# A two-layer hybrid encoder on eight cores: all engines ordered by a list scheduler, a token-major residual, linear chunked retention, a block form of the 31-tap convolution, and feed-forward groups of 512

## The chip, the cores and the metric

The kernel runs on all eight cores of one Trainium2 chip. Every core works on two of the sixteen sequences and runs the same program; no core talks to another. The metric is the device time of the slowest core in microseconds (us).

Executions come in states. In many of them some cores, often a pair or a whole die (cores 0 to 3 are die 0, 4 to 7 are die 1), are granted a lower TensorE clock than the others for some milliseconds, and the run is longer. Such a run is called slow; a run in which no die was held back is called fast. In a slow run the other die is often undisturbed. Two kinds of number are therefore compared in this text: fast runs with fast runs, and the spans of the cores of an undisturbed die. The runs were made on several chips. Undisturbed dies of the kernel before took about 12390 to 12450 us on all of them, so the spans can be compared across chips. The engines are PE (TensorE), DVE (VectorE), ACT (ScalarE), POOL (GpSimd) and SP (the queue that issues most transfers).

## The reference, cut to what matters

```python
D_MODEL, SEQ, DEPTH, CHUNK, D_FF = 1024, 2048, 2, 64, 4096     # 16 sequences in all

def hybrid_mixer(h, ...):
    q, k, v, g_ret, sc_b, sc_c, sc_x, cf_in, gate_logits = jnp.split(h @ w_in, split_at, axis=-1)
    # A: retention, 4 heads, keys 128 wide, values 256 wide. Weight of key m for query n:
    #    gamma_h^|n-m| in the same chunk of 64, gamma_h^(n-m) for earlier chunks, 0 for later ones
    o = head_norm(chunkwise_retention(rotary(q), rotary(k), v))
    y_a = (silu(g_ret) * o) @ w_ret_o
    # B: short gated convolution, 3 taps
    y_b = (sc_b * causal_depthwise_conv(sc_c * sc_x, sc_conv_w)) @ w_sc_o
    # C: conformer module: GLU, depthwise convolution of 31 taps, layer norm, silu
    u = causal_depthwise_conv(glu_a * sigmoid(glu_b), cf_dw_w) + cf_dw_b
    y_c = silu(layer_norm(u)) @ w_cf_o
    return (g0 * y_a + g1 * y_b + g2 * y_c) @ w_o               # g: sigmoid gates per channel

for l in range(DEPTH):
    x = x + 0.5 * rms_norm(swiglu_ffn(rms_norm(x, g[0]), ffn1_w_gu[l], ffn1_w_down[l]), g[1])
    x = x + rms_norm(hybrid_mixer(rms_norm(x, g[2]), ...), g[3])
    x = x + 0.5 * rms_norm(swiglu_ffn(rms_norm(x, g[4]), ffn2_w_gu[l], ffn2_w_down[l]), g[5])
```

Inputs and outputs are float32. Both kernels multiply in bfloat16 and accumulate in float32.

## The kernel before

The kernel is written by hand, one stage after the other. Each engine executes its instructions in the order in which the program makes them. Activations are kept feature-major (channels on the partitions, tokens along the rows), so a sum over channels needs a matmul with a matrix of ones. The parts that the argument touches:

```python
# sum of squares over channels: ACT squares, PE adds over the partitions with ones
def ssq_bank(srcs):
    pb = bank()
    for i, (ap, b) in enumerate(srcs):
        sq = sqbuf()                                              # two buffers
        P.op("act", lambda e: e.activation(out=sq.ap, in_=ap, func=AF.Square), ...)      # line 283
        P.mm_group([lambda pe: pe.matmul(pb.ap, lhsT=ONESB.ap, rhs=sq.ap, ...)], ...)    # line 284
    return pb

# feed-forward in 16 groups of 256 hidden channels; gate_up of the next step is issued before down of this one
for i, (g, t) in enumerate(steps):
    if i + 1 < len(steps):
        g2, t2 = steps[i + 1]
        gate_up(i + 1, g2, t2, wts[g2][0], wts[g2][1])
    down(i, g, t, wts[g][2])        # 8 banks, each added to the sum by DVE, 128x512 (line 379)
    if g == NG - 1:
        postnorm_tile(...)          # residual, sum of squares, and the next block's norm, at once

# retention: every pair of a 128-key tile and a 512-query tile; q and k are also projected a second
# time with their halves swapped, for the rotary embedding
for ib in range(T):
    for jt in range(4 * ib + 4):
        ...   # scores 128x512, DVE multiplies by the decay table, two matmuls with V

# 31-tap convolution: one diagonal 128x128 weight per tap
P.mm_group([(lambda pe, k=k: pe.matmul(pcv.ap, lhsT=DG[:, k, :], rhs=UG[:, t*TT+k:t*TT+k+TT],
                                       start=(k == 0), stop=(k == 30))) for k in range(31)], ...)  # line 731
```

The residual is transposed in float32 on entry (line 807) and on exit (line 822).

Of the kernel before, what the change touches and what calls it, by code (L numbers as in the profile page):

```python
# [10 lines left out]
ALU = mybir.AluOpType  # L11

S = 2048
D = 1024
C = 8
T = 4
TT = 512
NSEQ = 2
# [4 lines left out]
DK = 128  # L23
O_Q, O_K, O_V, O_GR, O_SCB, O_SCC, O_SCX, O_GA, O_GB, O_GATE = 0, 512, 1024, 2048, 3072, 4096, 5120, 6144, 7168, 8192
BIGD = 1.0e5

P_NG = 0
P_SCW = P_NG + L * 6 * C
P_CFW = P_SCW + L * 3 * C
P_CFB = P_CFW + L * 31 * C  # L30
P_LNG = P_CFB + L * C
# [4 lines left out]
NPAR = P_ID + 128  # L36
# [6 lines left out]
class Buf:  # L43
    __slots__ = ("w", "r", "dsem", "dcnt")

    def __init__(self):
        self.w = None
        self.r = {}
        self.dsem = None
        self.dcnt = 0  # L50

class TB:
    __slots__ = ("ap", "b")

    def __init__(self, ap, b=None):
        self.ap = ap
        self.b = b if b is not None else Buf()

class XSt:
    __slots__ = ("ap", "bs")  # L60

    def __init__(self, ap):
        self.ap = ap
        self.bs = [Buf() for _ in range(C)]

class Prog:
    def __init__(self, nc):
        self.nc = nc
        self.engs = {"pe": nc.tensor, "dve": nc.vector, "act": nc.scalar, "pool": nc.gpsimd, "sp": nc.sync}
        self.sem = {k: nc.alloc_semaphore(f"s_{k}") for k in self.engs}  # L70
        self.cnt = {k: 0 for k in self.engs}
        self.waited = {k: {} for k in self.engs}
        self.nsem = 0
        self.dma_toks = []

    def _wait(self, e, tok):
        sem, val = tok
        if e == "pe" and sem is self.sem["pe"]:
            return
        key = id(sem)  # L80
        if self.waited[e].get(key, 0) >= val:
            return
        self.engs[e].wait_ge(sem, val)
        self.waited[e][key] = val

    def deps(self, e, reads, writes):
        for b in reads:
            if b.w is not None:
                self._wait(e, b.w)
        for b in writes:  # L90
            if b.w is not None:
                self._wait(e, b.w)
            for t in b.r.values():
                self._wait(e, t)

    def commit(self, tok, reads, writes):
        k = id(tok[0])
        for b in reads:
            o = b.r.get(k)
            if o is None or o[1] < tok[1]:  # L100
                b.r[k] = tok
        for b in writes:
            b.w = tok
            b.r = {}

    def op(self, e, fn, reads=(), writes=()):
        self.deps(e, reads, writes)
        ins = fn(self.engs[e])
        self.cnt[e] += 1
        ins.then_inc(self.sem[e], 1)  # L110
        tok = (self.sem[e], self.cnt[e])
        self.commit(tok, reads, writes)
        return tok

    def mm_group(self, fns, reads=(), writes=()):
        e = "pe"
        self.deps(e, reads, writes)
        ins = None
        for fn in fns:
            ins = fn(self.engs[e])  # L120
        self.cnt[e] += 1
        ins.then_inc(self.sem[e], 1)
        tok = (self.sem[e], self.cnt[e])
        self.commit(tok, reads, writes)
        return tok

    def dma(self, q, out, in_, reads=(), writes=()):
        self.deps(q, reads, writes)
        tgt = writes[0] if writes else reads[0]
        if tgt.dsem is None:  # L130
            tgt.dsem = self.nc.alloc_semaphore(f"d{self.nsem}")
            self.nsem += 1
        tgt.dcnt += 16
        self.engs[q].dma_start(out=out, in_=in_).then_inc(tgt.dsem, 16)  # L134
        tok = (tgt.dsem, tgt.dcnt)
        self.commit(tok, reads, writes)
        self.dma_toks.append(tok)
        return tok

    def retire(self, bufs):  # L140
        toks = []
        for b in bufs:
            if b.w is not None:
                toks.append(b.w)
            toks += list(b.r.values())
        for e in self.engs:
            for t in toks:
                self._wait(e, t)

    def barrier(self):  # L150
        toks = [(self.sem[k], self.cnt[k]) for k in self.engs if self.cnt[k] > 0] + self.dma_toks
        for e in self.engs:
            for t in toks:
                self._wait(e, t)
        self.dma_toks = []

def build(nl=L, nseq=NSEQ, stop=None):
# [5 lines left out]

    x_d = din("x", [NSEQ, S, D])
    pos_d = din("pos", [NSEQ, S], I32)
    par_d = din("par", [128, NPAR])
    wtab_d = din("wtab", [128, 1408])
    wd = {n: din(n, WSHAPES[n]) for n in WNAMES}
    out_d = nc.dram_tensor("out", [NSEQ, S, D], F32, kind="ExternalOutput").ap()
    xs_d = nc.dram_tensor("xs", [NSEQ, C, 128, S], F32, kind="Internal").ap()  # L170
    xsb = [[Buf() for _ in range(T)] for _ in range(NSEQ)]
    outb = [[Buf() for _ in range(T)] for _ in range(NSEQ)]
# [5 lines left out]
    Hb = [[Buf() for _ in range(T)] for _ in range(C)]  # L178
    RA = sb("RA", [128, 16384], F32)
    ACC = RA.rearrange("p (c n) -> p c n", c=C)  # L180
    RAb16 = RA.bitcast(BF16)
    M = RAb16[:, 0:16384].rearrange("p (c n) -> p c n", c=C)
    U = RAb16[:, 16384:32768].rearrange("p (c n) -> p c n", c=C)
    ACCb = [[Buf() for _ in range(T)] for _ in range(C)]
    Mb = [[ACCb[c // 2][(c % 2) * 2 + t // 2] for t in range(T)] for c in range(C)]
    Ub = [[ACCb[4 + c // 2][(c % 2) * 2 + t // 2] for t in range(T)] for c in range(C)]
    R2 = sb("R2", [128, 8192], F32)
    R2b16 = R2.bitcast(BF16)
    NSLOT = 6
    RING = sb("RING", [128, NSLOT, 2048], BF16)  # L190
    ringb = [Buf() for _ in range(NSLOT)]
    XST = XSt(sb("XST", [128, C, TT], F32))
    PAR = TB(sb("PAR", [128, NPAR], F32))
    WTAB = TB(sb("WTAB", [128, 1408], F32))
    DTAB = TB(sb("DTAB", [128, 1408], F32))
    IDB = TB(sb("IDB", [128, 128], BF16))
    ONESB = TB(sb("ONESB", [128, 128], BF16))
    SQ = [TB(sb(f"SQ{i}", [128, TT], BF16)) for i in range(2)]
    HNB = [TB(sb(f"HNB{i}", [128, TT], BF16)) for i in range(4)]
    ST = [TB(sb(f"ST{i}", [128, TT], F32)) for i in range(4)]  # L200
    AC = [TB(sb(f"AC{i}", [128, TT], F32)) for i in range(3)]
    ACTB_raw = [sb(f"ACTB{i}", [128, 2, TT], BF16) for i in range(2)]
    ACTBb = [[Buf(), Buf()] for _ in range(2)]
    PT = [TB(ACTB_raw[0][:, 0, :], ACTBb[0][0]), TB(ACTB_raw[0][:, 1, :], ACTBb[0][1]), TB(ACTB_raw[1][:, 0, :], ACTBb[1][0])]
    PS = [TB(nc.alloc_psum_tensor(f"ps{i}", [128, TT], F32).ap()) for i in range(8)]

    all_out = []
    ctr = {"bank": 0, "sq": 0, "st": 0, "ac": 0, "pt": 0, "ring": 0}
    rot = {"banks": list(range(8))}

    def bank():
        lst = rot["banks"]
        i = lst[ctr["bank"] % len(lst)]
        ctr["bank"] += 1
        return PS[i]

    def rotbuf(lst, key):
        i = ctr[key] % len(lst)
        ctr[key] += 1
        return lst[i]  # L220

    def sqbuf():
        return rotbuf(SQ, "sq")

    def stbuf():
        return rotbuf(ST, "st")

    def acbuf():
        return rotbuf(AC, "ac")

    def ptbuf():
        return rotbuf(PT, "pt")

    def pcol(off):
        return PAR.ap[:, off:off + 1]
# [4 lines left out]
    IDENT = PAR.ap[:, P_ID:P_ID + 128]  # L240

    P.dma("sp", PAR.ap, par_d, writes=[PAR.b])
    P.dma("sp", WTAB.ap, wtab_d, writes=[WTAB.b])
    P.op("dve", lambda e: e.tensor_copy(out=IDB.ap, in_=IDENT), reads=[PAR.b], writes=[IDB.b])
    P.op("dve", lambda e: e.memset(ONESB.ap, 1.0), writes=[ONESB.b])

    def wslot():
        i = ctr["ring"] % NSLOT
        ctr["ring"] += 1
        return i  # L250
# [4 lines left out]
    def load_unit(pieces, a, bcols):  # L255
        i = wslot()
        view = RING[:, i, 0:a * bcols].rearrange("p (a b) -> p a b", a=a)
        for (c0, n, src) in pieces:
            P.dma("pool", view[:, :, c0:c0 + n], src, writes=[ringb[i]])
        return TB(view, ringb[i])  # L260

    def proj(w, col0, t, pb, src=H, srcb=Hb):
        P.mm_group([
            (lambda pe, k=k: pe.matmul(pb.ap, lhsT=w.ap[:, k, col0:col0 + 128], rhs=src[:, k, tsl(t)],  # L264
                                       start=(k == 0), stop=(k == C - 1)))
            for k in range(C)], reads=[w.b] + [srcb[k][t] for k in range(C)], writes=[pb.b])
# [38 lines left out]
    def load_x(seq, t, xst=None):  # L305
        xst = xst or XST
        if xst is XST:
            carve(XST.bs, "XST")
# [626 lines left out]
```

## Time and profile before

| what | before |
|---|---|
| timed runs at the start | 12808, 13064, 13017 us, median 13017 |
| profiled execution, slowest core | 12585.9 us; die 0 12404 to 12421, die 1 12548 to 12586 at a lower clock |
| PE busy | 88% |
| DVE busy, ACT busy | 52%, 23% |
| 512-wide matmuls in the program | 47104 |
| 256-wide matmuls; float32 transposes | 2048; 512 |

These are the lines of the page of the kernel before that show the limit: the span, the busy time of the engines, the busy tenths of PE in forty slices of the span, and the chain of waits that ended last, as shares of the span by engine.

```profile
span 12585.9 us, 150523 instructions; the slowest of 8 cores (12403.9 to 12585.9 us)
...
PE 11053.0 (88%) x48695; PEld 4960.2 (39%) x49664; DVE 6505.7 (52%) x10794; ACT 2872.7 (23%) x4545; POOL 750.9 (6%) x884
...
PE   4988898899898899889689889988989988998897
...
PE 82%; DVE 7%; ACT 5%; issue 3%; DMA 2%; DVEq 0%; ACTq 0%; SPq 0%; POOL 0%; another core or an unknown queue 0%; POOLq 0%
```

The chain runs through PE for 82% of the span. A busy PE is not yet a PE at full rate, however. The next view has stretches of 200 us of the kernel before: busy time of each engine with the number of its instructions, then the granted TensorE clock (1.00 is full), the share of the DMA engines and GB/s. Weight loads (PEld) are counted completely, so they tell the rate.

```profile
core 4: us, PE busy (x) PEld busy (x) DVE busy (x) ACT busy (x) POOL busy (x), PEclk, DMA share, GB/s
800.00:1000.00 200.00, 145.31 (x558) 57.63 (x567) 129.03 (x202) 69.68 (x107) 13.88 (x16) 0.80 0.43 89
2600.00:2800.00 200.00, 199.05 (x911) 90.66 (x927) 119.15 (x194) 23.32 (x39) 12.36 (x15) 1.00 0.30 39
3000.00:3200.00 200.00, 158.60 (x646) 65.84 (x657) 129.96 (x205) 59.73 (x92) 8.48 (x12) 0.85 0.37 85
```

In the middle of a feed-forward block (2600 to 2800 us) 927 weight loads pass in 200 us: 215.7 ns for each 512-wide matmul. This is the same as the Trainium skill gives for one matmul ("TensorE: Matmul & The Clock Gate", Back-to-back issue gap: N/2.4 + 2.5 ns), and here it is the sustained rate. Where a block ends (800 and 3000 us) only 567 and 657 pass: PE idles and its granted clock is down too, at 0.80 and 0.85.

The waits of PE in the kernel before name who is to blame. The columns are: who waits, for whom; us in total, times, the longest. This is core 4, the slowest.

```profile
PE ps L284 <- ACT SQ L283: 667.0, 519, 19.7
PE ps L471 <- ACT SQ L470: 125.8, 21, 10.1
PE ps L372 <- ACT AC L362: 122.5, 16, 8.0
PE ps L607 <- DVE ACTB L603: 120.8, 67, 7.1
```

The largest is the sum of squares for the RMS norm: ACT squares one 128x512 piece and PE adds it, in turns. On core 0, which belongs to the undisturbed die, all waits of PE add up to 1420 us.

Two groups of the kernel before matter later. Columns: line, engine, operation, output and inputs, count; busy us and mean ns; idle time before and who ended it.

```profile
L379 DVE TENSOR_TENSOR RA<-ps,RA 128x512 f32<-128x512 f32 x3840 | 2333.6, 678 | 0.0
...
L731 PE MATMUL ps<-R 128*128 128x512 bf16 x3880 | 895.3, 385 | 34.7 <-DVE R L723 29.2 <-issue 0.9
```

The first is the sum over feed-forward groups on DVE, the second the convolution on PE (3968 in the program; some matmul records are missing).

### The profile page before, as it was taken

The page shows a single profiled execution, that of the slowest core. Times are in us where ns is not written, and L with a number is a line of the kernel's source. Part 1 is how long each engine was busy: PE and PEld are TensorE (multiplying, and loading weights), DVE is VectorE, ACT ScalarE, POOL GpSimd, SP SyncE. Part 2 cuts the span into 40 slices and gives each one's busy share as a digit, 9 for nine tenths or more (in the row PEclk, how much of TensorE's full clock was granted, in tenths as well). Part 3 has the DMA queues.
Part 4 walks back from the last instruction along what each step waited for, and adds up shares of the span by engine and source line. Part 5 has one row for each costly group of instructions (what it writes and reads, how often), then busy time and mean ns, then how long its engine had stood idle before and what let it go on. Part 6 is the DMA issues. An engine that isn't in the chain of part 4 may idle for free.

```text
span 12585.9 us, 150523 instructions; the slowest of 8 cores (12403.9 to 12585.9 us)
## 1 busy us (share of the span) xinstructions
PE 11053.0 (88%) x48695; PEld 4960.2 (39%) x49664; DVE 6505.7 (52%) x10794; ACT 2872.7 (23%) x4545; POOL 750.9 (6%) x884
## 2 busy tenths in 40 slices
PE   4988898899898899889689889988989988998897
PEld 2434443344343444334334334433434433443343
DVE  1666443456566653445456664335556665424455
ACT  2123212311212311331221331133131133113212
POOL 0000010000000010000000001000000000100000
PEclk7999999899998999989899899998989989898887
DMA  4323231333333232233332323223223232312222
GB/s 105 45 54 46 31 36 12 74 41 51 64 44 72 27 33 24 26 78 74 86 55 43 72 27 33 25 26 74 39 70 50 44 56 31 36 14 37 61 36 62
DMA packets 936848, 602.28 MB, mean 48 GB/s; under 512 B 475040, under 2 KB 786336, under 8 KB 936096
## 3 DMA queue, kind: packets, MB, share of 16 engines
q0 software_dynamic: 816896, 335.60, 23.3%
q1 hardware_dynamic: 119200, 257.00, 6.0%
q8 instruction: 430, 7.05, 0.2%
q14 instruction: 322, 2.64, 0.1%
HBM read 810.64 MB, written 117.44 MB: 74 GB/s over the span
## 4 chain that ended last, share of the span: by engine, by line
PE 82%; DVE 7%; ACT 5%; issue 3%; DMA 2%; DVEq 0%; ACTq 0%; SPq 0%; POOL 0%; another core or an unknown queue 0%; POOLq 0%
PE ps L264 54%; PE ps L372 14%; PE ps L731 6%; ACT SQ L283 2%; PE ps L284 2%; PE ps L558 2%; PE ps L607 2%; DVE AC L338 1%; DVE R L341 1%; DMA RING<-w_in 1%; PE ps L585 1%; DVE ACTB L603 1%; DMA XST<-x 1%; DVE AC L740 1%; ACT L649 0%
## 5 line engine op out<-in xcount | busy, mean ns | idle before, releaser
L264 PE MATMUL ps<-H,RING 128*128 128x512 bf16 x27100 | 6315.9, 388 | 35.6 <-DMA RING<-w_in 3.3
L264 PEld LDWEIGHTS ps<-H,RING 128*128 128x128 bf16 x27648 | 2755.5, 100 | 3427.7 <-issue 502.7
L379 DVE TENSOR_TENSOR RA<-ps,RA 128x512 f32<-128x512 f32 x3840 | 2333.6, 678 | 0.0
L372 PE MATMUL ps<-ACTB,RING 128*128 128x512 bf16 x8052 | 1896.6, 387 | 131.0 <-ACT AC L362 122.5
L364 DVE TENSOR_TENSOR ACTB<-ps,AC 128x512 bf16<-128x512 f32 x1024 | 706.2, 691 | 2316.0 <-PE ps L264 2225.2
L362 ACT ACTIVATE AC<-ps 128x512 f32<-128x512 f32 x1024 | 609.6, 597 | 4154.8 <-PE ps L264 4145.0
L372 PEld LDWEIGHTS ps<-ACTB,RING 128*128 128x128 bf16 x8192 | 810.5, 99 | 1131.8 <-issue 253.0
L284 PE MATMUL ps<-SQ,ONESB 128*128 128x512 bf16 x747 | 353.7, 483 | 683.7 <-ACT SQ L283 667.0
L731 PE MATMUL ps<-R 128*128 128x512 bf16 x3880 | 895.3, 385 | 34.7 <-DVE R L723 29.2
L264 PE MATMUL ps<-RA,RING 128*128 128x512 bf16 x3000 | 741.6, 388 | 47.5 <-ACT RA L744 43.3
L731 PEld LDWEIGHTS ps<-R 128*128 128x128 bf16 x3968 | 390.3, 98 | 519.6 <-issue 86.9
L603 DVE SCALAR_TENSOR_TENSOR ACTB<-ps,DTAB 128x512 bf16<-128x512 f32 x640 | 412.9, 689 | 252.2 <-PE ps L585 139.9
L134 POOL DMA_DIRECT2D RING<-w_in x384 | 336.2, 877 | 3295.3 <-PE ps L264 1544.2
L607 PE MATMUL ps<-ACTB,R 128*128 128x512 bf16 x1252 | 394.4, 403 | 124.9 <-DVE ACTB L603 120.8
L723 DVE TENSOR_TENSOR R<-ps,AC 128x512 bf16<-128x512 f32 x128 | 88.1, 691 | 800.9 <-ACT AC L722 800.7
L134 POOL DMA_DIRECT2D RING<-ffn_w_gu x256 | 227.6, 890 | 4558.7 <-PE ps L264 4466.5
L497 ACT ACTIVATE AC<-ps 128x512 f32<-128x512 f32 x384 | 228.8, 597 | 1109.4 <-PE ps L264 1109.3
L264 PEld LDWEIGHTS ps<-RA,RING 128*128 128x128 bf16 x3072 | 305.3, 99 | 422.3 <-issue 104.7
L284 PEld LDWEIGHTS ps<-SQ,ONESB 128*128 128x128 bf16 x768 | 77.2, 101 | 953.1 <-issue 945.7
L503 DVE TENSOR_TENSOR AC<-ps,AC 128x512 f32<-128x512 f32 x256 | 176.9, 691 | 531.9 <-ACT AC L497 531.9
L338 DVE SCALAR_TENSOR_TENSOR AC<-RA,PAR,ST 128x512 f32<-128x512 f32 x384 | 286.6, 746 | 246.0 <-ACT ST L275 157.2
L712 DVE TENSOR_SCALAR R<-IDB,PAR 128x128 bf16<-128x128 bf16 x992 | 260.5, 263 | 106.4 <-DVE R L712 4.8
(108 smaller groups left out, 6242.9 us busy)
## 6 DMA issues: line engine op xcount, KB each, us to landing
RING<-ffn_w_gu POOLq DMA_DIRECT2D x256, 512.0 KB, 8.0
R<-xs SPq DMA_DIRECT2D x44, 2048.0 KB, 12.8
xs<-R SPq DMA_DIRECT2D x40, 2048.0 KB, 8.0
RING<-w_in POOLq DMA_DIRECT2D x288, 256.0 KB, 4.5
RING<-ffn_w_down POOLq DMA_DIRECT2D x128, 512.0 KB, 5.2
XST<-xs SPq DMA_DIRECT2D x12, 2048.0 KB, 10.1
XST<-x SPq DMA_DIRECT2D x8, 2048.0 KB, 15.5
RING<-w_in POOLq DMA_DIRECT2D x32, 512.0 KB, 7.3
```

The source lines that it names most:

```text
L134: self.engs[q].dma_start(out=out, in_=in_).then_inc(tgt.dsem, 16)
L264: (lambda pe, k=k: pe.matmul(pb.ap, lhsT=w.ap[:, k, col0:col0 + 128], rhs=src[:, k, tsl(t)], start=(k == 0), stop=(k == C - 1)))
L284: P.mm_group([lambda pe, sq=sq, i=i: pe.matmul(pb.ap, lhsT=ONESB.ap, rhs=sq.ap, start=(i == 0), stop=(i == n - 1))], reads=[sq.b, ONESB.b] ...
L338: P.op("dve", lambda e, ap=ap, tmp=tmp, c=c: e.scalar_tensor_tensor(out=tmp.ap, in0=ap, scalar=pcol(P_NG + (l * 6 + ni) * C + c), in1=rs.a ...
L362: P.op("act", lambda e, sg=sg, pg=pg: e.activation(out=sg.ap, in_=pg.ap, func=AF.Silu), reads=[pg.b], writes=[sg.b])
L364: P.op("dve", lambda e, sg=sg, pu=pu, jj=jj: e.tensor_tensor(out=ACTB_raw[ai][:, jj, :], in0=pu.ap, in1=sg.ap, op=ALU.mult), reads=[pu.b, ...
L372: (lambda pe, jj=jj: pe.matmul(pd.ap, lhsT=wdv.ap[:, jj, c * 128:(c + 1) * 128], rhs=ACTB_raw[ai][:, jj, :], start=(jj == 0), stop=(jj == 1)))
L379: P.op("dve", lambda e, pd=pd: e.tensor_tensor(out=ACC[:, c, tsl(t)], in0=pd.ap, in1=ACC[:, c, tsl(t)], op=ALU.add), reads=[pd.b, ACCb[c][ ...
L603: P.op("dve", lambda e, ps=ps, pt=pt, tab=tab, sc=sc: e.scalar_tensor_tensor(out=pt.ap, in0=ps.ap, scalar=float(sc), in1=tab, op0=ALU.mult ...
L607: (lambda pe, e_=e_, pt=pt: pe.matmul(OB[e_].ap, lhsT=VH[:, jt, e_ * 128:(e_ + 1) * 128], rhs=pt.ap, start=(jt == 0), stop=(jt == njt - 1)))
L712: P.op("dve", lambda e, k=k: e.tensor_scalar(out=DG[:, k, :], in0=IDB.ap, scalar1=pcol(P_CFW + (l * 31 + k) * C + c), scalar2=None, op0=AL ...
L731: (lambda pe, k=k: pe.matmul(pcv.ap, lhsT=DG[:, k, :], rhs=UG[:, t * TT + k:t * TT + k + TT], start=(k == 0), stop=(k == 30)))
```

## The change

The intent is to do less on PE and to have PE wait less. Nearly all of the kernel is new:

- **Order.** Operations are recorded first, with a planned duration and a place ("key") counted in PE time. A list scheduler then simulates all engines and buffer pools and issues on each engine what can start first, up to 60 us ahead of the oldest matmul that is left. Buffers are given out by the scheduler.
- **Residual.** It is token-major, so that ACT makes sums of squares along the row. bfloat16 transposes on PE turn the normed tile over; the matmuls with ones for the RMS norm and the float32 transposes go.
- **Retention.** Linear in the sequence: scores only inside a tile of 512 tokens, and a state carried from tile to tile. The second projection of q and k goes; DVE reads the swapped half instead.
- **Convolution.** 16 channels times 8 phases form a block of 128 rows, so that 31 taps are 5 block matmuls of 256 columns. The data goes to DRAM and comes back in this order, before and after.
- **Feed-forward.** 8 groups of 512 hidden channels in place of 16 of 256, and the sum is done 1024 wide.

The diff, cut to its core (the cuts are marked):

```diff
-        for jt in range(njt):                    # retention: all earlier key tiles
-            ps = s_banks.pop(jt)
-            P.op("dve", ... out=pt.ap, in0=ps.ap, scalar=float(sc), in1=tab, ...)
-            P.mm_group([... pe.matmul(OB[e_].ap, lhsT=VH[:, jt, ...], rhs=pt.ap, ...)])
+        psd = PS.tile(f32v(4, 128))              # scores within the tile of 512
+        ...
+        fns.append(lambda pe: pe.matmul(po.v[:, r, :], lhsT=qk.v[:, 0, ...], rhs=st.v..., ...))   # state
+        ...
+        P.op("dve", ... out=ns.v[:, 0:256], in0=st.v[:, 0:256], scalar=float(g512), in1=pst.v, ...)
 ...
-    (lambda pe, k=k: pe.matmul(pcv.ap, lhsT=DG[:, k, :], rhs=UG[:, t*TT+k:...])) for k in range(31)
+    P.op("dve", ... out=ug.v[:, :, t*64:(t+1)*64].rearrange("a p n -> a n p"),
+         in0=th.v.rearrange("a (n p) -> a n p", p=8), ...)                             # line 979
+    P.dma_op("sp", [scr1_d[c] <- ug]); P.dma_op("sp", [X <- scr1_d[c], 8 phases on the partitions])
+    (lambda pe, d=d: pe.matmul(pc.v[:, gi, :], lhsT=W.v[:, d, ...], rhs=X.v[:, g, 4-d:260-d])) for d in range(5)
 ...
+    P.op("act", ... out=u.v[...].rearrange("a (n p) -> a p n", p=8),                   # line 1041
+         in_=tmp.v[...].rearrange("a (p n) -> a p n", p=8), func=AF.Silu, ...), c_act(TT, 2), ...)
 ...
-        NG = DFF // 256
+        NG = DFF // 512
+        P.op("dve", ... out=ACC[:, b, :], in0=pd.v, in1=ACC[:, b, :], op=ALU.add)      # 128x1024, line 713
 ...
-            postnorm_tile(l, seq, npost, t, ...)
+            P.lag = 6.0
+            boundary(seq, b, ...)      # norm, residual, next norm; recorded 6 us later than its place
+            P.lag = 0.0
 ...
+    def _can(self, o, t, old, front):
+        if o.i != old and o.key > front + o.win:      # win is 60 us for computing instructions
+            return None
+        ...
+    P.schedule()
+    P.emit()
```

The scheduler takes an ACT instruction as 0.2 us + columns/1200, with 0.09 us more for each per-partition operand, and a DVE instruction as (150 + columns)/960 us.

## The prediction

> What bounds it now. The core is bound by the tensor engine and by the gaps in it. In the chain of waits PE holds 82% of the span of 12586 us, DVE 7%, ACT 5%. The windows show what a full stretch is: 927 weight loads in 200 us at clock 1.00, so 215.7 ns for a 512-wide matmul (the Trainium skill, "TensorE: Matmul & The Clock Gate", Back-to-back issue gap, has N/2.4+2.5 ns, the same); a burst of 32 256-wide ones took 3.7 us, 116 ns each. From the program: 47104 512-wide, 2048 256-wide and 512 float32 transposes (about 0.2 us): 10.16+0.24+0.10 = 10.50 ms. So about 2.1 ms of this core's span is no full-rate matmul work. The waits of PE give 1.45 ms of idling: 667 us on the squares of the RMS norm, about 570 us more on retention, layer norm, input and output transposes. The rest is a lower clock after gaps (windows at FFN ends: 0.80 to 0.85, 550 to 650 loads in 200 us) and a throttle on pairs of cores (4 and 5 after 10800 us, 6 and 7 early). DVE is busy 52%, DMA about 30%: neither bounds.
>
> What the change does to PE (counted in the built program). Swapped q/k projections go; retention becomes linear in chunks (S^2 scores gone); conv31 falls from 3968 512-wide matmuls to 1280 256-wide; ones-matmuls for RMS sums are replaced by 1536 128-wide bf16 transposes; float32 transposes go. Left: 38144 512-wide, 6528 256-wide, 64 384-wide, 2624 128-wide (I estimate 65 ns): 8.23+0.75+0.01+0.17 = 9.16 ms. All of the 1.34 ms saved is on the critical path.
>
> Gaps: sums of squares go to ACT with accumulation, each block's norm overlaps the next block's matmuls, and the order is chosen for all engines together. I expect 2.1 ms of losses to shrink to 0.4-0.6: start 50, retention 4x50 (many short groups, PSUM of 8 banks), layer norm tiles 16x10 (they fetch 128-byte pieces, 8192 per tile: at the 57 ns per packet that the software queue's 23.3% share implies, 29 us on 16 engines against some 45 us of matmuls), FFN ends 8x10.
>
> DVE: the FFN accumulation drops from 3840x678 ns = 2.33 ms to 896 1024-wide adds, estimated 1.22 us each (158+1067 ns): 1.1 ms. With norm, weight building and head scaling I estimate 5.0 ms in all. ACT about 2.2 ms. Neither is critical, except in the last FFN group (22 us DVE against 20.7 us PE per tile).
>
> Time. 9.16 + 0.5 = 9.7 ms undisturbed on the chip. Timed runs of before were 12.8 to 13.06 ms, 2 to 4% over its profile, so I add the throttle: the same page says the die falls to 13/16 under dense all-core matmuls; this trace shows it only part of the time. A quarter of the matmul work at 13/16 costs 9.16x0.23x0.25 = 0.5 ms; a denser kernel should meet it at least as often. Predicted 10150 us, range 9650 to 10950. Faster by over 2%: 0.97; within 2%: 0.02; slower: 0.01.
>
> What would show it: 47.2 thousand weight loads; full windows still at 927 loads; PE's waits below 400 us; no window at FFN ends under 0.9 clock; retention stage under 300 us per pass; DVE near 5.0 ms. Wrong if: windows at 0.81 cover most of the span (then 11 ms or more); layer-norm fetches take over 45 us per tile; the static order, made with modelled durations, stalls PE where a real DMA is later; 128-wide transposes cost over 100 ns.

## The result, and the profile after

| | runs (us) | median | fast runs |
|---|---|---|---|
| before | 12808, 13064, 13017, 12561, 12438, 12980 | 12893.8 | 12561.5, 12437.5 |
| after | 10207, 10739, 9931, 10203, 9922, 9939 | 10071.2 | 9931.0, 9921.5, 9939.2 |

The ratio of fast runs is 0.7945, with a 95% interval of 0.785 to 0.804. Ratios in this text are the mean time of one kernel's fast runs over the mean of the other's fast runs of the same rounds, so they are not quite the ratio of the medians that are quoted. The two fast runs of the kernel before differ by 1% here. On another chip, later, the ratio was 0.7989 (0.7955 to 0.8023), from fast runs before of 12420.0 and 12428.8 us; that is the cleaner figure. The spans of undisturbed dies are 12404 to 12421 us before and 9909 to 9930 us after.

These are the same lines of the page of the changed kernel.

```profile
span 9930.0 us, 121598 instructions; the slowest of 8 cores (9909.0 to 9930.0 us)
...
PE 9272.8 (93%) x47232; PEld 4541.0 (46%) x47232; DVE 4692.7 (47%) x5226; ACT 2620.8 (26%) x3807; POOL 1005.6 (10%) x1268
...
PE   8998998899999899799999989979999989897999
...
PE 82%; DVE 6%; ACT 5%; issue 4%; DMA 3%; POOL 1%; DVEq 0%; ACTq 0%; another core or an unknown queue 0%; SPq 0%; POOLq 0%
```

PE is busy 93% instead of 88%, in a span that is 2.5 ms shorter than that of an undisturbed core before. The chain has the same 82% of PE as before; it is a share of a shorter span, and it says that there is still something to be had.

How much of the gain is less work, and how much fewer losses? The page and the program give both, with the times of one matmul that the traces show at full clock: 215.7 ns for 512 columns, 109 ns for 256 (a burst of 32 took 3.49 us) and 55 ns for a transpose of 128 (8 took 0.44 us).

| | before | after |
|---|---|---|
| 512-wide | 47104 x 215.7 ns = 10.16 ms | 38144 x 215.7 ns = 8.23 ms |
| 256-wide | 2048 x 109 ns = 0.22 ms | 6528 x 109 ns = 0.71 ms |
| the rest | 512 float32 transposes, about 0.1 ms (estimate) | 64 of 384 and 2624 of 128: 0.15 ms |
| full-rate work | 10.49 ms | 9.09 ms |
| undisturbed span | 12.41 ms | 9.92 ms |
| losses (the difference, unrounded) | 1.93 ms | 0.83 ms |

So work fell by 1.39 ms and losses by 1.10 ms. Of the losses, PE's waits fell from 1420 to 644 us on core 0. Most of the rest is a lower granted clock while PE works: on core 0 the clock records of the traces hold only 1.00 and 0.50, with 0.50 for 1726 us before and 601 us after, and where PE was busy this cost 0.38 and 0.12 ms. It falls in the same stretches as the waits, as the windows of the changed kernel show. Columns are as before.

```profile
core 7: us, PE busy (x) PEld busy (x) DVE busy (x) ACT busy (x) POOL busy (x), PEclk, DMA share, GB/s
600.00:800.00 200.00, 169.36 (x922) 87.42 (x921) 120.01 (x131) 67.13 (x97) 34.08 (x46) 0.91 0.50 119
1600.00:1800.00 200.00, 149.27 (x720) 68.31 (x720) 102.57 (x131) 130.40 (x133) 16.11 (x23) 0.86 0.24 73
2000.00:2200.00 200.00, 199.91 (x925) 89.87 (x924) 69.58 (x57) 19.46 (x19) 14.07 (x17) 1.00 0.37 48
```

The middle of a feed-forward block is as before (924 loads at clock 1.00). The end of a block (600 to 800 us) is at 0.91 in place of 0.80 to 0.85. The weakest stretch is new: 1600 to 1800 us is the layer norm of the conformer branch, with PE busy 149 of 200 us. The waits of PE in the changed kernel say why:

```profile
PE ps L909 <- ACT F L1041: 277.5, 16, 19.7
PE ps L637 <- DVE F L634: 131.4, 41, 15.0
PE ps L996 <- DMA F<-scr: 90.6, 28, 4.2
```

Line 1041 is the Silu after the layer norm, 634 is the scaled tile that PE then transposes at the end of a block, and the third is the convolution's data on its way back from DRAM. Together they are 500 us of the 639 us on this core, core 7. The 16 waits for Silu are one in each of the 16 tiles (four tiles in each of four mixer passes), up to 19.7 us. One tile, on PE in the timeline (start, us, engine, line, what; in brackets the idle time before it and who ended it):

```profile
1611.72 16.50 PE L909 MATMUL ps<-F,RING 128*128 128x512 bf16 x64 [12.90 <-ACT F L1041]
```

and on ACT in the timeline of the same stretch:

```profile
1596.23 9.44 ACT L1041 ACTIVATE F<-F,PAR 128x512 bf16<-128x512 f32 x4
```

Four Silu instructions take 9.44 us. The groups of the changed kernel show that these are out of the ordinary, as is one on DVE:

```profile
L713 DVE TENSOR_TENSOR RA<-ps,RA 128x1024 f32<-128x1024 f32 x896 | 1095.9, 1224 | 748.5 <-PE ps L705 748.1
...
L1041 ACT ACTIVATE F<-F,PAR 128x512 bf16<-128x512 f32 x128 | 331.9, 2670 | 22.0 <-DVE F L1038 14.5 <-DVE SM L625 1.8
...
L979 DVE SCALAR_TENSOR_TENSOR F<-F,ps 128x512 bf16<-128x512 f32 x128 | 310.8, 2428 | 43.8 <-ACT F L978 38.1 <-DVE F L979 0.5
```

Line 713 is the sum over feed-forward groups: 896 times 1224 ns in place of 3840 times 678 ns, less than half. Lines 1041 and 979 write 512 columns of two bytes in steps (of 16 bytes on ACT, of 512 bytes on DVE) and take 2670 and 2428 ns, while the scheduler planned them at 0.2 + 512/1200 + 2x0.09 = 0.81 us and (150 + 512)/960 = 0.69 us. Those are the two instructions that the block form of the convolution needs for its change of order.

### The profile page after: what moved, and what is told of

It reads as the page before. It is cut to its first block, busy times and chain, and to the rows that moved or that the text cites. A ratio compares the mean times of both kernels' runs of the same rounds, so it can differ in the third digit from the quotient of the medians.

```text
span 9930.0 us, 121598 instructions; the slowest of 8 cores (9909.0 to 9930.0 us)
## 1 busy us (share of the span) xinstructions
PE 9272.8 (93%) x47232; PEld 4541.0 (46%) x47232; DVE 4692.7 (47%) x5226; ACT 2620.8 (26%) x3807; POOL 1005.6 (10%) x1268
## 4 chain that ended last, share of the span: by engine, by line
PE 82%; DVE 6%; ACT 5%; issue 4%; DMA 3%; POOL 1%; DVEq 0%; ACTq 0%; another core or an unknown queue 0%; SPq 0%; POOLq 0%
PE ps L606 50%; PE ps L705 17%; PE ps L909 7%; ACT F L1041 2%; DVE F L979 2%; PE ps L1067 2%; PE ps L996 2%; PE ps L810 1%; DMA F<-scr 1%; PE ps L817 1%; DMA scr<-F 1%; ACT F L623 1%; PE ps L637 1%; DVE F L802 1%; DMA RING<-ffn_w_gu 1%
## 5 line engine op out<-in xcount | busy, mean ns | idle before, releaser
L606 PE MATMUL ps<-H,RING 128*128 128x512 bf16 x25600 | 5669.2, 380 | 68.2 <-DVE F L1076 16.8
L705 PE MATMUL ps<-RING,F 128*128 128x512 bf16 x8192 | 1817.6, 379 | 16.2 <-DVE SM L625 4.7
L699 DVE TENSOR_TENSOR F<-ps,F 128x1024 bf16<-128x1024 f32 x512 | 626.5, 1224 | 2286.9 <-PE ps L606 2280.6
L697 ACT ACTIVATE F<-ps 128x1024 f32<-128x1024 f32 x512 | 525.3, 1026 | 3879.6 <-PE ps L606 3852.4
L713 DVE TENSOR_TENSOR RA<-ps,RA 128x1024 f32<-128x1024 f32 x896 | 1095.9, 1224 | 748.5 <-PE ps L705 748.1
L705 PEld LDWEIGHTS ps<-RING,F 128*128 128x128 bf16 x8192 | 787.3, 98 | 998.4 <-issue 94.8
L909 PE MATMUL ps<-RA,RING 128*128 128x512 bf16 x2048 | 482.5, 379 | 0.0
L627 POOL TENSOR_TENSOR SM<-SM,MHALF 128x1 f32<-128x1 f32 x384 | 270.0, 707 | 1885.7 <-DVE SM L625 1885.1
L1041 ACT ACTIVATE F<-F,PAR 128x512 bf16<-128x512 f32 x128 | 331.9, 2670 | 22.0 <-DVE F L1038 14.5
L979 DVE SCALAR_TENSOR_TENSOR F<-F,ps 128x512 bf16<-128x512 f32 x128 | 310.8, 2428 | 43.8 <-ACT F L978 38.1
```

The source lines that it names most:

```text
L606: P.mm([(lambda pe, k=k: pe.matmul(out(), lhsT=w.v[:, k, col0:col0 + 128], rhs=H[:, k, tsl(t)], start=(k == 0), stop=(k == C - 1))) for k ...
L627: P.op("pool", lambda e: e.tensor_tensor(out=ss.v[:, 1:2], in0=ss.v[:, 1:2], in1=MHALF[:, 0:1], op=ALU.pow), 0.7, [ss, MHALFb], [ss])
L697: P.op("act", lambda e, sg=sg, pg=pg: e.activation(out=sg.v, in_=pg.v, func=AF.Silu), c_act(1024), [pg], [sg])
L699: P.op("dve", lambda e, sg=sg, pu=pu, a=a: e.tensor_tensor(out=a.v, in0=pu.v, in1=sg.v, op=ALU.mult), c_dve(1024), [pu, sg], [a])
L705: P.mm([(lambda pe, h=h, j=j, pd=pd, acts=acts: pe.matmul(pd.v[:, h * 512:(h + 1) * 512], lhsT=acts[j // 2].v[:, j % 2, s * 128:(s + 1) * ...
L713: P.op("dve", lambda e, pd=pd, b=b: e.tensor_tensor(out=ACC[:, b, :], in0=pd.v, in1=ACC[:, b, :], op=ALU.add), c_dve(1024), [pd, ACCb[b]], ...
```

## The experiments

Twelve kernels were run. The theories were these; the expectations call some of them by letters:

- Less PE work, on the critical path, gives its full time (tested on two parts: the convolution and the swapped projection); the rival is that it is given back as waits.
- Theory A: the remaining losses are the long stepped instructions themselves. Its rival: not their length but the scheduler's wrong plan for them.
- Theory D: the order found by the scheduler, not the arithmetic, makes most of the fall of the losses.
- Theory F: buffers that come free late keep transposes and transfers waiting.
- Wide feed-forward groups spare DVE time; whether this is worth anything, as DVE is not the limit, is open.

A span "undisturbed" is the span of the cores of a die that had the clock of the fast runs. The changed kernel has 9909 to 9930 us by this measure, with 644 us of PE waits on core 0.

| run | undisturbed span (us) | PE waits, core 0 (us) | against after (us) |
|---|---|---|---|
| e1_contig | 9721 to 9745 | 461 | about -190 |
| e2_truecost | 9776 to 9797 | 540 | about -135 |
| e3_inorder | 12321 to 12333 | 2611 | about +2400 |
| e4_conv31 | 10257 to 10278 | 329 | about +345 |
| e5_ffn256 | 10175 to 10215, with throttle bursts | 780 | about +230 without them |
| e6_best, c_best | 9338 to 9349 | 162, 164 | about -575 |
| e7_swapproj | 10113 to 10125 (die 1) | 630 | about +200 |
| e8_pool | 9812 to 9833 | 553 | about -95 |
| e9_interleave | 9748 to 9756 (die 0 of one run; 9751 and 9752 on cores 0 and 1 of another) | 506 (in a throttled run) | about -170 |
| b1_defer (the kernel before, edited) | none clean | not comparable | not comparable |
| c_after | 9911 to 9921 | | 0 |

### e1_contig: the two stepped writes become stepped reads

```diff
-  out=ug.v[:, :, t*64:(t+1)*64].rearrange("a p n -> a n p"), in0=th.v.rearrange("a (n p) -> a n p", p=8), ...
-  in1=pa.v.rearrange("a (n p) -> a n p", p=8), ...
+  out=ug.v[:, :, t*64:(t+1)*64], in0=th.v.rearrange("a (n p) -> a p n", p=8), ...
+  in1=pa.v.rearrange("a (n p) -> a p n", p=8), ...
...
-  out=u.v[:, ...].rearrange("a (n p) -> a p n", p=8), in_=tmp.v[:, i, :].rearrange("a (p n) -> a p n", p=8), ...
+  out=u.v[:, ...].rearrange("a (n p) -> a n p", p=8), in_=tmp.v[:, i, :].rearrange("a (p n) -> a n p", p=8), ...
```

The result is the same; only the order in which the elements are walked differs: outputs are now written one after the other, and the four-byte inputs are read in steps.

> The new kernel with the iteration order of two operations swapped: the Silu of the layer norm and the GLU product of the conformer branch write contiguous runs and read strided, where they wrote two-byte elements one by one at a stride and took 2656 and 2428 ns instead of the 0.7 us of their contiguous likes. Theory A (the strided write is the cost, and it is what the tensor engine waits for): both fall under 1.3 us, PE's wait for the Silu falls from 277 us to under 80 us, total PE waits from 657 to under 450 us, time 9930 -> 9600 to 9700 us. Rival B (any stride, read or written, costs the same): both stay above 2 us and the time stays within 1%. Rival C (PE waits for the chain of the layer norm, not for the Silu's duration): the operations get shorter, the wait stays above 200 us.

The groups of this run:

```profile
L1041 ACT ACTIVATE F<-F,PAR 128x512 bf16<-128x512 f32 x128 | 160.0, 1265 | 16.3 <-DVE F L1038 8.8 <-DVE SM L625 1.9
L979 DVE SCALAR_TENSOR_TENSOR F<-F,ps 128x512 bf16<-128x512 f32 x128 | 138.1, 1079 | 71.9 <-ACT F L978 66.4 <-ACT F L1002 0.6
```

and its waits of PE, on core 0:

```profile
PE ps L637 <- DVE F L634: 123.1, 40, 13.6
PE ps L909 <- ACT F L1041: 111.5, 16, 9.2
```

Both instructions are less than half as long, the wait for Silu fell from 277 to 111 us, and the span by about 190 us. All six runs of this kernel were slow ones, so the span is read from their undisturbed die; five of the six had one, with 9721 to 9745 us. Theory A holds in the main, though this run also brings the true durations nearer to the planned ones, so that it does not separate length from plan; the next run changes the plan alone. Its size was less than expected, because a read in steps is not free: the same two instructions without any stepping, in the run e4_conv31 below, took 811 and 688 ns, against 1265 and 1079 here.

### e2_truecost: leave the instructions, tell the scheduler their true length

```diff
-  ... c_dve(TT), [th, pa], [ug])
+  ... 2.43, [th, pa], [ug])
...
-  ... func=AF.Silu, ...), c_act(TT, 2), [tmp, PARb], [u])
+  ... func=AF.Silu, ...), 2.66, [tmp, PARb], [u])
```

> The new kernel, same instructions, but the list scheduler is told the measured durations of the Silu (2.66 us, it assumed 0.81) and of the GLU product (2.43 us, it assumed 0.69). If the wrong plan is the cost (the engine has time for these operations, they are only placed too late), PE's wait for the Silu falls from 277 us to under 100 us and the time to about 9700 us. If the durations themselves are the cost, the wait stays above 200 us and the time within 1% of 9930 us. I expect something between: about 150 us of the wait left, 9800 us.

Fast runs were 9794.5 and 9798.0 us, about 135 us less than the changed kernel's, with no instruction made shorter. The waits of PE in this run, on core 0:

```profile
PE ps L637 <- DVE F L634: 265.4, 52, 15.2
PE ps L909 <- ACT F L1041: 105.4, 16, 8.7
```

The wait for Silu fell to 105 us, as far as with the shorter instruction. The scheduler now puts other matmuls into the time. The wait of the transposes for DVE rose from 125 to 265 us on core 0 in return. So a good part of the layer norm's loss was not the length of Silu but a plan that did not know it: the rival of theory A is right too. The two gains are not to be added.

### e3_inorder: the same program in program order

```diff
-  if o.i != old and o.key > front + o.win:
+  if o.i != old and o.key > front + (o.win if o.dma is not None else 0.0):
```

Computing instructions may no longer be issued ahead of the oldest matmul's place; transfers still may. The work on every engine is the same.

> The new kernel with its freedom of order taken away: compute operations go in program order (only the small fixed lags of the block norms remain), transfers still run ahead as before. Theory D (list scheduling is what removed most of the gaps): PE's waits rise from 657 us to 1500 us or more, and the time to 11000 us or more (+1 ms). Rival E (the gaps went with the ones-matmuls and the short block chains, program order would do): waits below 1000 us, time below 10400 us. PE's instructions stay 47232.

The waits of PE on core 0:

```profile
PE ps L637 <- DVE F L634: 665.2, 142, 15.8
PE ps L996 <- DMA F<-scr: 423.2, 32, 15.5
PE ps L705 <- DVE F L699: 414.9, 256, 2.3
```

The run has the same 47232 matmuls, but an undisturbed span of 12321 to 12333 us: all but 80 to 100 us of the whole change is gone. The waits are 2611 us, which is more than the 1420 us of the kernel before: that one had a pipeline made by hand, with the next step's gate and up projections issued before this step's down projections (the wait of line 705 for 699 is that loss). So theory D holds, and it was under-estimated: I had expected +1 ms, and +2.4 ms came. The new way to make the norm does not by itself remove its wait: in program order the transposes wait 665 us for the normed tile, as long as the matmuls with ones waited for the squares before (649 us). New mathematics in the order in which it is written down is worth next to nothing here; the 1.39 ms of saved work shows only when the order fills the gaps. What a pipeline made by hand would have got out of the new mathematics was not run.

### e4_conv31: the convolution back to 31 diagonal weights

```diff
-  ug.v[...] stepped; scr1_d[c] <- ug; X <- scr1_d[c]; 8 groups x 5 matmuls of 256; scr2_d[c] <- Y in 8 phases
+  DG = F4.tile(bfv(31, 128), 2)                  # DVE: identity times each tap
+  for t in range(T):
+      P.mm([(lambda pe, k=k: pe.matmul(pc.v, lhsT=DG.v[:, k, :], rhs=ug.v[:, t*TT+k:t*TT+k+TT], ...)) for k in range(31)], ...)
+  P.dma_op("sp", [(lambda: scr2_d[c], lambda: Y.v)], ...)      # natural order; Silu without steps
```

> The new kernel with the 31-tap convolution done as before: 31 diagonal 128x128 weights per channel block, 3968 512-wide matmuls in place of 1280 256-wide ones, in natural token order, so that the trips through memory for the phase layout and the strided writes go too. PE work rises by 3968*0.216-1280*0.109 = 717 us (numbers of the trace). If the block form saves what its matmuls say, the time rises by about that less the waits that go with the phase layout (277 us on the Silu, 91 us on the transfers): 9930 + 717 - 330 = 10300 us. If the whole 717 us shows (10650 us), the waits are not of the phase layout. If it rises by less than 150 us, the block form was worth little.

This puts back 3968 x 215.7 - 1280 x 109 ns = 716 us of PE work. The undisturbed die took 10257 to 10278 us (10300 was expected): about 345 us more than the changed kernel, and about 540 us more than e1_contig. PE's waits fell from 644 to 329 us (Silu 75 in place of 277, the wait for the convolution's data gone), and the mean granted clock rose from 0.970 to 0.986. So the block form saves PE 716 us and gives half of it back, in waits that it brings itself. With the stepped writes mended (e1_contig), it keeps about three quarters.

### e5_ffn256: feed-forward in groups of 256 again

```diff
-  NG = DFF // 512 ... for pr in range(2): ...
+  NG = DFF // 256 ... for pr in range(1): ...
-  front = pe_keys[pe_ptr][0] if pe_ptr < len(pe_keys) else inf
+  front = pe_keys[min(pe_ptr, len(pe_keys) - 1)][0]
```

The number of matmuls is unchanged, and the sum over groups on DVE doubles. The second edit was needed, because with these groups the scheduler otherwise runs out of buffers after the last matmul and stops. Not shown: the making of the rotary tables, which is recorded inside the groups, is moved to the corresponding groups.

> The new kernel with FFN groups of 256 hidden columns instead of 512, as before: the same matmuls, but the vector engine adds to the accumulator 15 times instead of 7 per block, 1920 adds of 1.224 us instead of 896, +1.25 ms of vector work (4.69 -> about 5.95 ms). (One line of the scheduler is mended too: after the last matmul it no longer takes the buffer reserve.) Theory: accumulation is off the critical path, so the time stays within 1% of 9920 us on an undisturbed die. Rival: in the last group of each FFN the vector engine (about 21 us per tile against 10.4 us of matmuls) becomes the limit; then each of the 8 FFN ends loses about 40 us and the time rises by about 300 us, with PE waits on the block norm (the line of the transposes) well above 131 us.

The only run without a disturbed die was 10216 us, and it had throttle bursts: two windows of 200 us with PE all but full had clocks of 0.86 and 0.85 and 795 and 790 weight loads in place of 927, which is 58 us of matmuls. Net of these it is about 230 us slower than the changed kernel. DVE was busy 5868 us (57%) in place of 4693 us; the 1920 sums alone keep it busy for 2.22 ms. PE's timeline on core 0 at the end of a block:

```profile
789.11 1.01 PE L637 MATMUL ps<-IDB,F 128*128 128x128 bf16 x8 [5.16 <-DVE F L634]
795.29 1.01 PE L637 MATMUL ps<-IDB,F 128*128 128x128 bf16 x8 [5.17 <-DVE F L634]
801.47 1.01 PE L637 MATMUL ps<-IDB,F 128*128 128x128 bf16 x8 [5.17 <-DVE F L634]
```

One transposed tile comes every 6.18 us, and PE waits 5.16 us for DVE each time. DVE is not the limit on average, but in the last group of a block it has the sum, the post-norm, the residual and the next norm at once, and there it sets the pace. The wait of PE for line 634 is 225 us in place of 125 on core 0. The narrower group makes the same end work fall on half the matmuls. So wide groups pay, but by an amount that the averages of DVE hide. The expected size was about 300 us.

### e7_swapproj: project q and k a second time, as the kernel before did

```diff
+  wsw = wtile([q and k columns of the head with their halves swapped], C, 256)
+  psw = PS.tile(f32v(2, TT), 2); proj(... wsw ...) for i in range(2)
-  for o_, i_ in ((0, 64), (64, 0)): t2.v[o_:o_+64] = pqk.v[i_:i_+64] * sin[i_:i_+64]
+  t2.v = psw.v * sin                     # sign of the table turned round
```

> The new kernel with the projections of the swapped halves of q and k put back (1024 more 512-wide matmuls, 1024*0.216 = 221 us), and the rotary product read from them in one vector instruction in place of two half-height ones of 1.22 us (128 fewer, 64 more: 78 us less of vector work). If retention is bound by the tensor engine, all of the 221 us shows: 9920 -> 10140 us on an undisturbed die. If retention waits for the vector engine or for buffers, part of it is hidden: less than 150 us.

It adds 1024 matmuls of 512 columns, 221 us. On die 1, which had the clock of the changed kernel's fast runs (0.970), the span was 10113 to 10125 us: 200 us more. For this projection, PE work saved is time saved almost one for one, unlike in the convolution. The rest of the retention, its linear form, was not put back.

### e8_pool: one ring buffer less, one working buffer more, no reserve

```diff
-  RING = P.pool("ring", ..., 10, 1024, 0);  F4 = P.pool("f4", ..., 9, 1040, 2)
+  RING = P.pool("ring", ..., 9, 1024, 0);   F4 = P.pool("f4", ..., 10, 1040, 0)
```

> The new kernel with only the buffers changed: 9 ring slots, 10 work buffers of 4 KB, none in reserve. Theory F (the wait of the transposes for the block norm, 131 us, and part of the waits for the convolution's transfers come from work buffers running out, so that neither the next matmuls nor the norm can be prepared): time 9920 -> about 9730 us, that wait below 60 us, the transfers' below 60 us. Rival G (it is the vector engine's chain of four operations per block): the wait stays at 100 us or more, time above 9850 us.

Two of the waits of PE on core 0:

```profile
PE ps L996 <- DMA F<-scr: 86.7, 28, 3.7
PE ps L637 <- DVE F L634: 57.2, 29, 14.6
```

The gain is about 95 us, half of the expected 190. The wait of the transposes fell from 125 to 57 us, so these had in fact mostly waited for buffers. The wait for the convolution's data hardly moved (90 to 87 us), so that was not buffers. Theory F is right for one and wrong for the other.

### e9_interleave: the convolution between the pieces of the short convolution

```diff
-  conf_conv(l)
-  short_conv(l)
+  cc, sc = conf_conv(l), short_conv(l)      # now generators, with a yield after each step
+  for c in range(C):
+      next(cc); next(sc); next(cc)          # GLU and store; short convolution; the block matmuls
```

> The new kernel with only the record order of two stages changed: one channel block of the conformer convolution, then one pair of the short convolution, in turn, so that matmuls which need no trip through memory lie near those that do. If the windows of the convolution stage (clock 0.93 to 0.96, 91 us of waits for the transfers) lose time because nothing else is near enough in the order, the waits for the transfers go below 15 us and the time falls to about 9720 us on an undisturbed die. If the transfers themselves are the limit, less than 50 us is gained.

The wait of PE for the convolution's data, 90 us on core 0 of the changed kernel, is no longer in the list of waits, so there it was the distance in the program between store and use. One run had an undisturbed die with 9748 to 9756 us, and in another two undisturbed cores took 9751 and 9752 us: about 170 us less than the changed kernel. The profiled execution was throttled on both dies (10369 to 10593 us) and only its waits and the states of its cores are used. The throttle does not explain the lost wait: in the profiled run of c_after, core 0 was throttled too (clock 0.92) and the wait was 74 us.

### e6_best and c_best: the parts together

```diff
   the edits of e1_contig, e8_pool and e9_interleave, with planned durations of 1.08 and 1.27 us, and
-  ... c_act(D) + 0.1 ...                              # sum of squares on ACT
+  ... c_act(D) + 0.2 ...
-  for b in range(NB): first_h(0, b, g0)               # start: all 16 blocks, then the first matmuls
+  for b in range(4): first_h(0, b, g0)                # the others inside the first group
+  P.lag = -30.0; us = layer_norm_tile(l, t); P.lag = 0.0
```

> The new kernel with all that I think is left to gain: contiguous writes (as in e1_contig), true durations told to the scheduler, the conformer convolution recorded alternately with the short convolution, layer norms favoured by 30 us, the ring of weights cut from 10 to 9 slots for a tenth 4 KB work buffer and no reserve there, and the first activations fetched tile by tile. Same matmuls (47232). If the waits that are left in the new kernel are of order and buffers, PE waits fall from 650 us to under 250 us and the undisturbed die runs in 9350 to 9450 us, 5% below the new kernel. If they are of latencies that no order hides, it stays above 9600 us.

> The same kernel as e6_best, timed beside c_after. Fast runs about 9345 to 9380 us, ratio to fast runs of c_after 0.942 to 0.946. If a denser kernel meets the throttle more often or longer, its fast runs are rarer than those of c_after and the medians lie closer than the fast runs.

> The new kernel unchanged, on the chip and in the rounds of c_best, to compare the two in like states. About 9920 us on an undisturbed die, as before; in a slow state anything from 10200 to 11600 us, since every matmul of a throttled core takes 1/0.81 of its time.

c_best is the same kernel as e6_best, run again on another chip beside the changed kernel (c_after) and the kernel before. The page of c_best:

```profile
span 9348.7 us, 121711 instructions; the slowest of 8 cores (9340.6 to 9348.7 us)
...
PE 9168.8 (98%) x47232; PEld 4519.5 (48%) x47232; DVE 4489.9 (48%) x5234; ACT 2461.4 (26%) x3803; POOL 1045.0 (11%) x1268
...
PE   8998999999999999999999999999999999999999
...
PE 93%; DVE 3%; issue 2%; POOL 1%; ACT 0%; DMA 0%; another core or an unknown queue 0%; DVEq 0%; SPq 0%; POOLq 0%; ACTq 0%
```

and its two largest waits of PE, on core 0:

```profile
PE ps L637 <- DVE F L634: 61.5, 29, 15.6
PE ps L900 <- DVE F L896: 28.1, 24, 5.4
```

Fast runs of c_best were 9350.0 and 9353.1 us, of c_after 9929.5 and 9922.1 us, of the kernel before 12420.0 and 12428.8 us. Against before, c_best is at 0.7527 (0.7494 to 0.7559) and c_after at 0.7989 (0.7955 to 0.8023); c_best over c_after is 9351.5/9925.8 = 0.942. Its chain holds 93% PE, its waits are 164 us (below 250 was expected), its mean clock is 0.994. It has the same 9.09 ms of full-rate work, so the losses are 0.25 ms in place of 0.83 ms. Three of its parts were measured alone (190, 95 and 170 us, 455 us of the 575); the start, the lead of the layer norm and the other planned durations were not run alone.

### b1_defer: the kernel before, with its norms put off

```diff
-  postnorm_tile(...)                     # at once after the last down projection of a tile
+  later.append((i + 1, post))            # post-norm one step later, the next norm two steps later
+  later.append((i + 2, pre))
```

The question was how much of the old losses a small change of order would have mended.

> The kernel before with only the order at the end of each FFN changed: the post norm of a tile is issued one step later and the next pre norm two steps later, so that the in-order queue of the tensor engine holds 48 to 96 other matmuls while the squares and the norm are made. Same instructions. If the gaps of the kernel before are gaps of order, PE's wait for the squares falls from 650 to about 400 us (the mixer's ends are left as they are), and the time of an undisturbed die from 12410 to about 12100 us. If the chain itself is too long for that, less than 100 us is gained.

It gave a wrong result (relative error 0.667): at the end of the first sequence the next sequence's tile is loaded into a buffer that a norm still pending had already filled. Both dies were throttled in parts, so the spans are not used either. What can be read on core 0, before its throttle began: the decay table of the third mixer pass starts at 7115.5 us in place of 7188.9 us, 73 us ahead after five feed-forward blocks, about 15 us for each. The wait for the squares fell from 649 to 482 us, but a new one on DVE (68 us) came, and the wait for the down projections' input rose from 123 to 185 us. Putting the norm off by a step or two is little. This run is inconclusive on how good an order the kernel before could have reached.

## Why the prediction was right or wrong

The prediction was 10150 us; 10071 us was measured, inside the range of 9650 to 10950. What bounds the kernel and what the change takes away were foreseen; that the number fell so near is partly luck, as the point on the throttle shows. Point by point:

- **What bounds the kernel: right.** PE's matmuls and the gaps in them. e7_swapproj (+221 us of matmuls, +200 us) shows it for the projection in the retention.
- **The matmul work: right.** 9.16 ms predicted, 9.09 ms from measured times; transposes took 55 ns, not the estimated 65, and 256-wide matmuls 109 ns, not 116.
- **"All of the 1.34 ms saved is on the critical path": nearly right for the swapped projection (200 of 221 us), half right for the convolution.** e4_conv31 shows that its 716 us of saved matmuls gave 345 us, because the block form brought stepped writes and a way through DRAM. About 0.45 ms of the saved work (the score tiles of retention and the matmuls with ones, by difference) was not tested by itself.
- **"Shrink to 0.4-0.6": the term that was mis-sized.** The losses are 0.83 ms, and the undisturbed span is 9.92 ms, not 9.7. "PE's waits below 400 us" is wrong as well: they were 628 to 644 us, according to the core.
- **The cause given for the layer norm's loss: wrong.** The prediction blamed the fetches in pieces of 128 bytes ("29 us on 16 engines"). These land quickly, as the list of transfers of the changed kernel shows (what, queue, count, KB each, median us from issue to landing):

```profile
F<-scr SPq DMA_DIRECT2D x128, 128.0 KB, 3.6
```

  Each tile has eight of these, and no wait of PE is for them; the wait for transfers in the list above is the convolution's. The layer norm lost 277 us, about 17 us for each of 16 tiles rather than 10, in the main to stepped writes of Silu that the prediction did not cost at all, and to the plan that took them for 0.81 us: e1_contig left 111 us of it, e2_truecost 105 us, and in c_best, which has both mended and the layer norm favoured, it is gone from the list of waits.
- **Start, retention, block ends: right.** The first 200 us have 758 weight loads on core 7, of which 128 are for transposes of 128: 143 us of full-rate work, so a loss of about 57 us (50 predicted). The first retention pass lasts from 737 to about 1017 us, 280 us, under the 300 predicted. Block ends have clocks of 0.91 and more, as predicted. The windows below 0.9 are layer norms.
- **DVE and ACT: DVE right, ACT too low.** 4.69 ms for DVE (5.0 predicted), with the sums of the feed-forward at 1.224 us (1.22 predicted) and 1.10 ms. ACT took 2.62 ms, not 2.2: the stepped Silu is 0.33 ms, and reading the row sums out after each square costs 0.12 ms in instructions of their own (188 to 195 ns each).
- **"Neither is critical, except in the last FFN group": wrong for ACT.** In the layer norm PE waited 277 us for Silu on ACT, more than for anything else. For DVE at the end of a feed-forward block the waits were 125 to 131 us, and e8_pool shows that more than half of that was buffers (57 us were left). That DVE can set the pace there is shown tile by tile only with narrower groups, in e5_ffn256.
- **The throttle: mis-sized the other way.** 0.45 ms was added to the undisturbed 9.7 ms. In the six runs the median is only 0.15 ms above the undisturbed 9.92 ms. So two errors cancelled: the undisturbed kernel is 0.22 ms slower than predicted, and the throttle took 0.3 ms less. This was luck: three of the six runs were slow, and the median lies midway between the slowest fast run (9939 us) and the quickest slow one (10203 us). On another chip the throttle took more: the median of c_after was 10617 us with a highest run of 11552 us. "A denser kernel should meet it at least as often" was not borne out in the counts: fast runs were 2 of 11 for before, 2 of 8 for c_after and 2 of 6 for c_best on one chip. These are few, and they do not show the contrary either.
- **"The static order, made with modelled durations, stalls PE": it came true**, though on an ACT instruction instead of a transfer (e2_truecost).

The largest thing that the prediction did not see is how the two parts hang together. It summed work saved and losses saved as if each could be had alone. e3_inorder shows that the new arithmetic in its own order is hardly faster than the kernel before (12.33 against 12.41 ms).

What stays open: how much a better order alone could have given the kernel before (b1_defer failed), how much the new mathematics would give with a pipeline made by hand, and the parts of c_best that were not run alone.

## What to carry to other kernels

When a kernel is bound by matmuls, count full-rate matmul time from the program and subtract it from an undisturbed span; what is left is the most that a better order can win, and here the losses fell by nearly as much as the work did (1.10 against 1.39 ms). A static scheduler is as good as its planned durations: compare them with the measured mean of every group, and look first at the instructions with stepped two-byte writes, which took more than three times as long as planned. A saving that needs a change of data order pays part of itself back, so cost the change of order as carefully as the matmuls.

## What the Trainium skill lacked or had wrong

- "TensorE: Matmul & The Clock Gate", Back-to-back issue gap: the formula N/2.4 + 2.5 ns, which this section calls isolated, is the sustained rate here: 215.7 ns for 512 columns over thousands of load and matmul pairs, 109 ns for 256 in bursts of 32, 55 ns for 128 in bursts of 8. The "sustained roofline" of the same section was met by no run: its 131 ns at 512 was not reached, and its 81 ns at 128 was undercut.
- The same page, Seeing it yourself, has a whole die go to 13/16 of the clock soon after a third core runs dense matmuls, and stay there while the load lasts. All eight cores ran dense at clock 1.00 through whole fast runs (mean 0.994 in c_best). Where the clock did fall to 0.81, it was mostly by pairs of cores: in the profiled run of e9_interleave, from 200 to 600 us, cores 0 and 6, and their neighbours 1 and 7, had 0.81 (1524 weight loads in 400 us, 262.5 ns each) while cores 2 and 4 had 1.00 (1849 and 1850 loads). Both pairs of a die can be down together for a time: in e4_conv31 core 4 had 0.80 and core 6 still 1.00 from 2000 to 2400 us, but from 4000 to 4400 us both had 0.81. The size of the step agrees with the page, the unit and the lasting do not.
- "Vector Engine (DVE) Microarchitecture Reference", 5.2 Measured stream behaviour on trn2, lists four-byte words only. Here, two-byte writes in steps of 512 bytes took 2428 ns for 128x512 (line 979), four-byte reads in steps of 32 bytes with writes in order took 1079 ns, and all in order 688 ns.
- "ScalarE: Activation LUTs" says nothing of stepped addresses. Silu of 128x512 took 2670 ns with two-byte writes in steps of 16 bytes, 1265 ns with four-byte reads in steps of 256 bytes, and 811 ns in order. The note on 16-byte lines in "SBUF — State Buffer" (Door 1: The DMA port swizzle) agrees in kind, but has no figure for either engine.
